# One decoder step on a Trainium2 core: two output tiles take turns, matmul by matmul, on one chunk of weights

## The chip, the cores and the metric

The kernel runs on one core of one Trainium2 chip. The metric is the device time of that core in microseconds; several executions are timed, and the median is given. Before the change it is 1397.88 us (3 runs, 1395.66 to 1398.28).

The engines in this text are TensorE (PE in the profile, with its weight loads as PEld), VectorE (DVE), ScalarE (ACT), GpSimd (POOL) and SyncE (SP), which issues most of the DMAs. PSUM is the memory into which TensorE adds; it is split into banks, and each accumulator of this kernel has a bank of its own.

## What is computed

One inference step of one decoder layer, for a prompt of 256 tokens and for 8 requests with 4 tokens each, 288 token columns in all. The model width is 2048, that of the feed-forward 5632.

```python
def layer(x, pos, ssm0, conv0, kbuf, vbuf, mk, mv, lp):
    mix, ssm_new, conv_new, k_new, v_new = mixer(rmsnorm(x, lp['norm_mix']), pos, ssm0, conv0, kbuf, vbuf, lp)
    x = x + mix
    x = x + cross_attn(rmsnorm(x, lp['norm_x']), mk, mv, lp)
    x = x + ffn(rmsnorm(x, lp['norm_ffn']), lp)
    return x, ssm_new, conv_new, k_new, v_new

def ffn(h, lp):
    return (jax.nn.silu(h @ lp['w_gate']) * (h @ lp['w_up'])) @ lp['w_down']
```

The mixer multiplies its input by `w_in`, and from the product come a gate, the inputs of a state-space scan (a causal convolution of four taps, then 16 heads with a state of 64 by 128 each) and queries, keys and values of a sliding-window attention with 16 heads. Both halves are joined and multiplied by `w_out`. The cross attention reads keys and values of 256 memory tokens. After the last layer comes a final norm. Everything is float32; besides the two outputs, the new states and caches are returned.

## The kernel before, in words

**Tiles.** Activations lie transposed: the 2048 channels are 16 tiles of 128 partitions, each with the 288 token columns. A matmul keeps a 128 x 128 slice of weights still and streams 288 columns of activations past it, into an accumulator `mm` of 128 x 288 in PSUM. float32 is reached by three matmuls of parts: weights and activations are each split into a rounded part (hi) and the rest (lo), and `mm3` (L164 to L168) adds lo·x_hi (L166), hi·x_hi (L167) and hi·x_lo (L168).

**Weights.** `wload` (L139 to L158) fetches a chunk of 128 x 1024 weights (512 KB) into a tile `raw` by SyncE's DMAs; ScalarE casts it to `hi` (L156), DVE subtracts to get `lo` (by the helper at L79). There are 3 buffers for raw, 4 for hi and 4 for lo. A chunk has four slices along the input channels (k) for two output tiles (m). In the chunks of the queries (`perm`), the two output tiles interleave in memory, and the split is done for each output tile apart, in two instructions of 512 columns each per engine; elsewhere one instruction splits the chunk.

**The order of the matmuls.** `gemm` takes accumulators for a pair of output tiles from a pool of four (`p_mm`) and has `gemm_w` (L179 to L189) go through the chunks:

```python
            for m in range(len(pss)):
                for k in range(n):
                    mm3(pss[m][:, :T], (hv[:, k, m * P:(m + 1) * P], lv[:, k, m * P:(m + 1) * P]), xs[k0 + k],
                        k0 + k == 0, k0 + k == nk - 1)
                if m == 0:
                    step(0)
```

So a full chunk gives 12 matmuls into the first accumulator, then 12 into the second. The next pair uses the other two accumulators. All large products go through it (input projection, output projection, cross attention's queries and output, feed-forward); only the memory keys and values call `mm3` themselves.

**Other work between them.** `later` puts a piece of work (a convolution, a part of the state-space scan, an attention step) into a queue with a due time, counted in chunks, and `step` (L127 to L132) emits what is due: once in the middle of a chunk, by `step(0)`, and once at its end. A scheduler then orders each engine's instructions by the priority of the place at which they were written; loads and splits are given a higher one, so that they run ahead.

**Places that the steps below touch.** `conv_pair` (L673 on) copies a tile of the input projection into a row with the old tail (L680 and L681 on GpSimd), scales it, and adds four taps (L82 on DVE); its tiles are called s, and the copy of the tail goes out as cc (L693, L694). `decay` makes masks m (L769 on DVE, a product at L79 on GpSimd). `ssd` makes four scaled copies of its input on GpSimd (L79, tiles s of 128 x 256), which `states` multiplies at L814 and L820. `sample_state` scales the old states (GpSimd, L79, tiles m from ld, 128 x 512). `residual` (L1011 on) adds a finished accumulator to the residual xT (DVE, L79), and squares the sum on ScalarE; at the very end, two tiles of squares wait in `tail` and are summed on TensorE by `final_sums` (L1275 to L1279). After that, TensorE transposes xT for the output (L118).

Of the kernel before, what the change touches and what calls it, by code (L numbers as in the profile page):

```python
# [15 lines left out]
P = 128  # L16
# [4 lines left out]
T = TP + TS  # L21
# [25 lines left out]
def tile_hymba_step(ctx: ExitStack, tc: tile.TileContext, I: dict, O: list, stop: int = 99):  # L47
    nc = tc.nc
# [3 lines left out]
    def tl(pool, shape, dt, tag):  # L52
        uid[0] += 1
        return pool.tile(shape, dt, name=f"{tag}_{uid[0]}", tag=tag)
# [20 lines left out]
    def acc():  # L75
        return tl(p_mm, [P, 512], F32, "mm")
# [49 lines left out]
    def step(n=1, part=False):  # L126
        clock[0] += n  # L127
        due = sum(t <= clock[0] for t, _, _ in pend)
        left = due // 2 if part else 0
        while pend and pend[0][0] <= clock[0] and (not part or due > left):  # L130
            due -= 1
            heapq.heappop(pend)[2]()  # L132
# [27 lines left out]
    def wslice(w, k0, nk, c0, ncol):  # L160
        v = w.rearrange("(k p) c -> p k c", p=P)
        return [(lambda r: r, v[:, k0:k0 + nk, c0:c0 + ncol])]

    def mm3(ps, w, x, start, stop):  # L164
        (wh, wl), (xh, xl) = w, x
        nc.tensor.matmul(ps, wl, xh, start=start, stop=False)  # L166
        nc.tensor.matmul(ps, wh, xh, start=False, stop=False)  # L167
        nc.tensor.matmul(ps, wh, xl, start=False, stop=stop)  # L168
# [5 lines left out]
    def gemm_part(pss, chunks, k0, nk, xs, ahead=AHEAD, perm=False):  # L174
        for pieces, n in chunks:
            gemm_w(pss, [wload(pieces, n, len(pss) * P, ahead, perm)], k0, nk, xs)
            k0 += n

    def gemm_w(pss, ws, k0, nk, xs):  # L179
        for hv, lv in ws:  # L180
            n = hv.shape[1]
            for m in range(len(pss)):
                for k in range(n):
                    mm3(pss[m][:, :T], (hv[:, k, m * P:(m + 1) * P], lv[:, k, m * P:(m + 1) * P]), xs[k0 + k],
                        k0 + k == 0, k0 + k == nk - 1)
                if m == 0:
                    step(0)
            k0 += n
        step(part=True)  # L189

    def gemm(chunks, nk, nm, xs, **kw):
        pss = [acc() for _ in range(nm)]
        gemm_part(pss, chunks, 0, nk, xs, **kw)
        return pss

    def kchunks(w, nk, c0, ncol, k_base=0):
        out = []
        k = 0
        while k < nk:
            n = min(1024 // ncol, nk - k)  # L200
            out.append((wslice(w, k_base + k, n, c0, ncol), n))
            k += n
        return out
# [116 lines left out]
    def ts(w=T, n=P, dt=F32):  # L320
        return tl(mxs, [P, 320], dt, "s")[:n, :w]
# [4 lines left out]
    def proj_in(c0, ncol):  # L326
        return gemm(kchunks(w_in, KC, c0, ncol), KC, ncol // P, xmix)

    # keys, values and the first queries
    wq = w_in.rearrange("(k p) c -> p k c", p=P)  # L330

    def q_chunk(rp, k0, nk=4):
# [74 lines left out]

    later(1, kv_natural)

    # dt path  # L410
    nat = ts(192).rearrange("p (c j h) -> p c j h", c=3, j=4)
    csrow = tc.dram_tile([16, T], F32, name="csrow")
    wdt = tl(p_ld, [P, 512], F32, "ld").rearrange("p (k h) -> p k h", h=32)
# [72 lines left out]
    later(1, dt_natural)  # L486
    later(7, dt_sums)

    # prompt sliding-window attention
    att = [(tl(p_xb, [P, T], F32R, "xb"), tl(p_xb, [P, T], F32R, "xb")) for _ in range(8)]  # L490
    qs = ts(256).rearrange("p (b r t) -> p b r t", r=8, t=4)
    mp = cst[:, C_MP:C_MP + 384]
# [69 lines left out]
        for m in range(2):  # L562
            swa_prompt(2 * rp + m, pq[m])

    # sample sliding-window attention
    def swa_sample():
        ms = cst[:, C_MS:C_MS + 144]
        kcT, vc = [], []
# [86 lines left out]
            cm.__exit__(None, None, None)  # L655
        return

    # state-space heads
    xc = [ts() for _ in range(12)]
    scT = ts().rearrange("p (c k) -> p c k", k=24)  # L660

# [178 lines left out]

        later(1, diag)

    # sample states
    bm = cst[:TS, C_BM:C_BM + 8]
    ssm = I["state_ssm"][0].rearrange("b (i f) p n -> i (f p) b n", f=2)
    osm = o_sssm[0].rearrange("b (i f) p n -> i (f p) b n", f=2)
# [79 lines left out]
        if jj % 2:  # L926
            later(4, lambda jj=jj: sample_state(jj // 2))

    # gate and group norm
    ymx = []  # L930

    def gate(i0, zzs, sqs):
# [21 lines left out]
    for g in range(2):  # L954
        sqs = ts()
        for zp in range(2):
# [7 lines left out]
            last = g == 1 and zp == 1  # L964
# [4 lines left out]
    def att_chunks(c0):  # L969
        chunks = []  # L970
        for j in range(2):
            pcs = []
            for g in range(2):
                r0 = 1024 + 512 * g + 256 * j
                pcs.append((lambda v, g=g: v[64 * g:64 * g + 64],
                            w_out[r0:r0 + 256, c0:c0 + 256].rearrange("(r d) c -> d r c", d=64)))
            chunks.append((pcs, 4))
        return chunks

    first = [[acc() for _ in range(2)] for _ in range(2)]  # L980
# [85 lines left out]
    for mp_ in range(8):  # L1066
        c0 = 256 * mp_
        if mp_ < 2:
            pss = first[mp_]
            gemm_part(pss, kchunks(w_out, 4, c0, 256, k_base=4), 12, KC, mix)  # L1070
        else:
            pss = gemm(att_chunks(c0) + kchunks(w_out, 8, c0, 256), KC, 2, mix)
# [5 lines left out]
    later(1, lambda: load_mem(2))  # L1078
    later(3, lambda: load_mem(3))

    # cross attention
    oT = [(tl(p_xb, [P, T], F32R, "xb"), tl(p_xb, [P, T], F32R, "xb")) for h in range(4)]
    qm = [ts(256).rearrange("p (b t) -> p b t", b=NB) for _ in range(4)]
    for h in range(4):
# [99 lines left out]
    for hp in range(2):  # L1184
# [6 lines left out]
        pss = gemm(kchunks(I["w_xq"][0], KC, 256 * hp, 256), KC, 2, xcs)  # L1191
# [37 lines left out]
    for w, o_ in ((I["w_xk"][0], o_pmk), (I["w_xv"][0], o_pmv)):  # L1229
        for hp in range(2):  # L1230
            pss = [acc() for _ in range(2)]
            for c in range(4):
                hv, lv = wload(wslice(w, 4 * c, 4, 256 * hp, 256), 4, 256)
# [30 lines left out]
    for mp_ in range(8):  # L1264
        pss = gemm(kchunks(I["w_xo"][0], 4, 256 * mp_, 256), 4, 2, oT)
# [1 line left out]
            residual(2 * mp_ + j, pss[j][:, :T], x3[2 * mp_ + j], V_F)  # L1267
    later(2, rstd_bcast)

    # feed-forward  # L1270
    NF = DFF // P
    NH = NF // 2

# [6 lines left out]
    for half in range(2):  # L1280
# [23 lines left out]
        for mp_ in range(8):  # L1304
            if half and mp_ == 7:
                later(3, lambda: final_sums(0, ssum))
            pss = gemm(kchunks(I["w_down"][0], NH, 256 * mp_, 256, k_base=half * NH), NH, 2, hs)
            for j in range(2):
                k = 2 * mp_ + j
# [5 lines left out]
                    if k == 0:  # L1315
                        act(rf[:, 13:14], xT[0][:, 0:1], AF.Sqrt, scale=0.0, bias=rf[:, 12:13])

    # final norm
    ydst = [o_yp[0, 0:P], o_yp[0, P:TP], o_ys.rearrange("b t d -> (b t) d")]
    ys = []  # L1320

# [108 lines left out]
```

## Time and profile before

| | before |
|---|---|
| median of 3 runs | 1397.88 us |
| lowest and highest | 1395.66 and 1398.28 us |
| span of the profiled execution | 1393.4 us |
| DMA | 241.17 MB, mean 173 GB/s |

The profile shows one execution of its own. For it no time beside its span is given; the span is the time from the first instruction to the last that the profiler recorded, and the median of the runs lies 4.48 us above it. An engine's busy time sums its instructions; since matmuls are pipelined, one begins before the one ahead of it has ended, and the spacing of starts tells more than the duration of one. PEclk is the clock that TensorE was granted as a share of full speed: 1.00 is 2.4 GHz and 0.50 is 1.2 GHz. In a timeline, the figure in brackets is the engine's idle time before the row, with what ended it.

### The profile page before, as it was taken

The numbers are of one execution on the slowest core, as the hardware profiler recorded it, in microseconds if no ns is written. First come the engines' busy times: TensorE is split into PE (matmuls) and PEld (weight loads), VectorE is DVE, ScalarE is ACT, GpSimd is POOL, SyncE is SP. The second block draws the span as 40 slices with busy tenths as digits, with TensorE's granted clock in tenths as the row PEclk, the third lists the DMA queues.
The fourth block names the chain that finished last, engine by engine and source line by source line (L and its number), as shares of the span: only waits on it lengthen the run. The fifth ranks groups of instructions, "written<-read, shape, count | busy, mean of one in ns | idle before, by whom it ended". The sixth has DMA issues, their size and how long they took to land.

```text
span 1393.4 us, 26184 instructions
## 1 busy us (share of the span) xinstructions
PE 1373.9 (99%) x10637; PEld 1338.3 (96%) x10637; DVE 809.1 (58%) x1341; ACT 635.1 (46%) x998; POOL 177.2 (13%) x273
## 2 busy tenths in 40 slices
PE   9899999999999999999999999999999999999997
PEld 8799988899998899999999999999999999999997
DVE  6777798766666559544544544444454554545554
ACT  6355776554555556433433433333343333434332
POOL 4311476403220113000000000000000000000110
PEclk9999999999999999999999999999999999999999
DMA  9655547667657745555555545555555555555552
GB/s 291 169 157 144 150 120 231 187 195 206 185 192 243 228 155 161 166 166 167 162 170 166 166 160 164 165 165 174 167 167 167 167 167 167 167 159 167 166 167 91
DMA packets 249856, 241.17 MB, mean 173 GB/s; under 512 B 12778, under 2 KB 240528, under 8 KB 249736
## 3 DMA queue, kind: packets, MB, share of 16 engines
q1 hardware_dynamic: 246120, 232.43, 54.9%
q0 software_dynamic: 3584, 7.06, 1.7%
q8 instruction: 83, 1.36, 0.4%
q14 instruction: 37, 0.30, 0.1%
q10 hardware_dynamic: 32, 0.01, 0.0%
HBM read 227.59 MB, written 11.85 MB: 172 GB/s over the span
## 4 chain that ended last, share of the span: by engine, by line
PE 87%; DVE 5%; DMA 2%; ACT 2%; issue 2%; POOL 0%; SPq 0%; DVEq 0%; ACTq 0%; POOLq 0%
PE mm L166 27%; PE mm L167 27%; PE mm L168 27%; PE ps L118 2%; DMA raw<-in_w_in_dram 2%; DVE lo L79 2%; DVE s L82 1%; ACT hi L156 1%; PE ps L511 1%; DVE xa L82 1%; DVE m L769 0%; PE ps L1134 0%; DVE s L79 0%; ACT L85 0%; ACT s L85 0%
## 5 line engine op out<-in xcount | busy, mean ns | idle before, releaser
L79 DVE TENSOR_TENSOR lo<-raw,hi 128x1024 fp32r<-128x1024 f32 (+1 forms) x413 | 483.0, 1172 | 472.7 <-ACT hi L156 466.3
L156 ACT CAST hi<-raw 128x1024 fp32r<-128x1024 f32 (+1 forms) x413 | 410.9, 998 | 547.4 <-PE mm L168 435.6
L166 PE MATMUL mm<-xa,lo 128*128 128x288 f32 x2016 | 601.2, 298 | 0.0
L167 PE MATMUL mm<-xa,hi 128*128 128x288 f32 x2016 | 597.5, 296 | 0.0
L168 PE MATMUL mm<-xa,hi 128*128 128x288 f32 x2016 | 591.0, 293 | 0.0
L166 PEld LDWEIGHTS mm<-xa,lo 128*128 128x128 f32 x2016 | 378.4, 188 | 4.7 <-issue 3.8
L168 PEld LDWEIGHTS mm<-xa,hi 128*128 128x128 f32 x2016 | 379.7, 188 | 0.7 <-issue 0.6
L167 PEld LDWEIGHTS mm<-xa,hi 128*128 128x128 f32 x2016 | 379.4, 188 | 1.0 <-issue 0.7
L79 POOL TENSOR_TENSOR ssum<-ssum,ls 128x288 f32<-128x288 f32 x43 | 46.9, 1091 | 880.0 <-ACT ls L85 879.1
L166 PE MATMUL mm<-ls,lo 128*128 128x288 f32 x512 | 152.0, 297 | 0.0
L168 PE MATMUL mm<-ls,hi 128*128 128x288 f32 x512 | 151.4, 296 | 0.0
L167 PE MATMUL mm<-ls,hi 128*128 128x288 f32 x512 | 151.1, 295 | 0.0
L167 PE MATMUL mm<-xb,hi 128*128 128x288 f32 x448 | 132.5, 296 | 0.0
L166 PE MATMUL mm<-xb,lo 128*128 128x288 f32 x448 | 132.1, 295 | 0.0
L168 PE MATMUL mm<-xb,hi 128*128 128x288 f32 x448 | 132.1, 295 | 0.0
L166 PEld LDWEIGHTS mm<-ls,lo 128*128 128x128 f32 x512 | 96.2, 188 | 0.1
L168 PEld LDWEIGHTS mm<-ls,hi 128*128 128x128 f32 x512 | 96.2, 188 | 0.0
L167 PEld LDWEIGHTS mm<-ls,hi 128*128 128x128 f32 x512 | 96.1, 188 | 0.1
L168 PEld LDWEIGHTS mm<-xb,hi 128*128 128x128 f32 x448 | 84.6, 189 | 0.2 <-DVE xb L79 0.2
L166 PEld LDWEIGHTS mm<-xb,lo 128*128 128x128 f32 x448 | 84.5, 189 | 0.1
L167 PEld LDWEIGHTS mm<-xb,hi 128*128 128x128 f32 x448 | 84.0, 188 | 0.1
L79 DVE TENSOR_TENSOR xT<-xT,mm 128x288 f32<-128x288 f32 x64 | 28.2, 448 | 39.1 <-PE mm L168 36.2
(304 smaller groups left out, 1211.3 us busy)
## 6 DMA issues: line engine op xcount, KB each, us to landing
raw<-in_w_gate_dram SPq DMA_DIRECT2D x88, 512.0 KB, 3.6
raw<-in_w_up_dram SPq DMA_DIRECT2D x88, 512.0 KB, 3.6
raw<-in_w_down_dram SPq DMA_DIRECT2D x80, 512.0 KB, 3.5
raw<-in_w_in_dram SPq DMA_DIRECT2D x43, 512.0 KB, 3.9
raw<-in_w_in_dram SPq DMA_DIRECT2D x34, 256.0 KB, 5.3
raw<-in_w_out_dram SPq DMA_DIRECT2D x32, 256.0 KB, 4.1
raw<-in_w_out_dram SPq DMA_DIRECT2D x16, 512.0 KB, 3.6
ld<-in_state_ssm_dram SPq DMA_DIRECT2D x16, 256.0 KB, 4.1
```

The source lines that it names most:

```text
L79: eng.tensor_tensor(out=out, in0=in0, in1=in1, op=op)
L82: nc.vector.scalar_tensor_tensor(out=out, in0=in0, scalar=s, in1=in1, op0=op0, op1=op1)
L118: nc.tensor.transpose(out, in_, ident[b:b + k, 0:k])
L156: nc.scalar.copy(h_, src)
L166: nc.tensor.matmul(ps, wl, xh, start=start, stop=False)
L167: nc.tensor.matmul(ps, wh, xh, start=False, stop=False)
L168: nc.tensor.matmul(ps, wh, xl, start=False, stop=stop)
L511: nc.tensor.matmul(pss[g][:, oc], qa[gs, qc], kT[gs, kc], start=True, stop=True)
```

## The change

In `gemm_w` the loop over the two output tiles goes inside: for each k and each of the three products, the matmul for the first accumulator is followed at once by the one for the second. The order of the three products for one accumulator, and its start and stop flags, stay. The queue's `step(0)` stood between the two output tiles; now it stands after the second of four values of k, again in the middle of the chunk. In a chunk with two values of k it stands after the first.

```diff
     def gemm_w(pss, ws, k0, nk, xs):
         for hv, lv in ws:
             n = hv.shape[1]
-            for m in range(len(pss)):
-                for k in range(n):
-                    mm3(pss[m][:, :T], (hv[:, k, m * P:(m + 1) * P], lv[:, k, m * P:(m + 1) * P]), xs[k0 + k],
-                        k0 + k == 0, k0 + k == nk - 1)
-                if m == 0:
+            for k in range(n):
+                xh_, xl_ = xs[k0 + k]
+                for w, x, first, last in ((lv, xh_, True, False), (hv, xh_, False, False), (hv, xl_, False, True)):
+                    for m in range(len(pss)):
+                        nc.tensor.matmul(pss[m][:, :T], w[:, k, m * P:(m + 1) * P], x,
+                                         start=first and k0 + k == 0, stop=last and k0 + k == nk - 1)
+                if k == (n - 1) // 2:
                     step(0)
             k0 += n
         step(part=True)
```

Behind these lines every line number grows by two (L814 becomes L816, L1277 becomes L1279). The scheduler moves other instructions with the matmuls; three places follow.

**TensorE, the last chunk of the last pair of output tiles.** mm_2607 and mm_2608 are the two accumulators, hi_2625 and lo_2626 the chunk's weights, ls the activations. Before:

```order
L166 MATMUL mm_2607_15543<-ls_2445_14266,lo_2626_15700 128x288
L167 MATMUL mm_2607_15543<-ls_2445_14266,hi_2625_15699 128x288
L168 MATMUL mm_2607_15543<-ls_2446_14267,hi_2625_15699 128x288
L166 MATMUL mm_2607_15543<-ls_2449_14276,lo_2626_15700 128x288
L167 MATMUL mm_2607_15543<-ls_2449_14276,hi_2625_15699 128x288
L168 MATMUL mm_2607_15543<-ls_2450_14277,hi_2625_15699 128x288
L166 MATMUL mm_2608_15544<-ls_2445_14266,lo_2626_15700 128x288
L167 MATMUL mm_2608_15544<-ls_2445_14266,hi_2625_15699 128x288
L168 MATMUL mm_2608_15544<-ls_2446_14267,hi_2625_15699 128x288
L166 MATMUL mm_2608_15544<-ls_2449_14276,lo_2626_15700 128x288
L167 MATMUL mm_2608_15544<-ls_2449_14276,hi_2625_15699 128x288
L168 MATMUL mm_2608_15544<-ls_2450_14277,hi_2625_15699 128x288
```

And now:

```order
L186 MATMUL mm_2607_15543<-ls_2445_14266,lo_2626_15700 128x288
L186 MATMUL mm_2608_15544<-ls_2445_14266,lo_2626_15700 128x288
L186 MATMUL mm_2607_15543<-ls_2445_14266,hi_2625_15699 128x288
L186 MATMUL mm_2608_15544<-ls_2445_14266,hi_2625_15699 128x288
L186 MATMUL mm_2607_15543<-ls_2446_14267,hi_2625_15699 128x288
L186 MATMUL mm_2608_15544<-ls_2446_14267,hi_2625_15699 128x288
L186 MATMUL mm_2607_15543<-ls_2449_14276,lo_2626_15700 128x288
L186 MATMUL mm_2608_15544<-ls_2449_14276,lo_2626_15700 128x288
L186 MATMUL mm_2607_15543<-ls_2449_14276,hi_2625_15699 128x288
L186 MATMUL mm_2608_15544<-ls_2449_14276,hi_2625_15699 128x288
L186 MATMUL mm_2607_15543<-ls_2450_14277,hi_2625_15699 128x288
L186 MATMUL mm_2608_15544<-ls_2450_14277,hi_2625_15699 128x288
```

The first accumulator's last matmul was the sixth from the end and is the second from the end now; in a chunk with four values of k it goes from the thirteenth from the end to the second. Behind these matmuls, the column sums of the second tile of squares (L1279 now) stand three transposes (L118) later than they did (L1277).

**TensorE, at the products of `states` in the mixer** (ps from s; xa, hi and lo belong to the input projection, cst is the identity). Before:

```order
L166 MATMUL mm_507_2525<-xa_15_136,lo_534_2651 128x288
L814 MATMUL ps_527_2637<-s_513_2560,s_434_2155 128x256
L820 MATMUL ps_529_2641<-s_434_2155,s_514_2562 128x128
L820 MATMUL ps_529_2641<-s_435_2156,s_515_2564 128x128
L820 MATMUL ps_529_2641<-s_434_2155,s_514_2562 128x128
L820 MATMUL ps_529_2641<-s_435_2156,s_515_2564 128x128
L167 MATMUL mm_507_2525<-xa_15_136,hi_533_2650 128x288
L168 MATMUL mm_507_2525<-xa_31_152,hi_533_2650 128x288
L118 MATMUL ps_535_2679<-cst_82,s_304_1495 128x128
```

And now:

```order
L186 MATMUL mm_507_2525<-xa_32_153,hi_542_2694 128x288
L186 MATMUL mm_506_2524<-xa_17_138,lo_543_2695 128x288
L186 MATMUL mm_507_2525<-xa_17_138,lo_543_2695 128x288
L816 MATMUL ps_527_2637<-s_513_2560,s_434_2155 128x256
L822 MATMUL ps_529_2641<-s_434_2155,s_514_2562 128x128
L822 MATMUL ps_529_2641<-s_435_2156,s_515_2564 128x128
L822 MATMUL ps_529_2641<-s_434_2155,s_514_2562 128x128
L822 MATMUL ps_529_2641<-s_435_2156,s_515_2564 128x128
L118 MATMUL ps_535_2679<-cst_82,s_304_1495 128x128
```

L814, which is L816 now, stood inside the chunk of hi_533 and lo_534, behind 934 large matmuls; it stands inside the next chunk (hi_542, lo_543) now, behind 944. The transposes of s_304 still follow behind 936 before, 944 now.

On DVE, the split of that next chunk, lo_543, has moved with it. The piece of the difference there (s_499 is the second convolution tile, m_522 a mask of the scan, xb the keys and values):

```order
-L79 TENSOR_TENSOR lo_534_2651<-raw_532_2649,hi_533_2650 128x1024
-L79 TENSOR_TENSOR xb_157_720<-ps_480_2359,xb_156_719 128x32
-L82 SCALAR_TENSOR_TENSOR s_499_2509<-s_498_2508,cwT_111,s_499_2509 128x312
-L769 TENSOR_SCALAR m_522_2590<-csb_519_2584,s_137_679 128x128
-L82 SCALAR_TENSOR_TENSOR s_499_2509<-s_498_2508,cwT_111,s_499_2509 128x312
+L79 TENSOR_TENSOR lo_543_2695<-raw_541_2693,hi_542_2694 128x1024
 L79 TENSOR_TENSOR xb_159_722<-ps_480_2359,xb_158_721 128x32
 L82 SCALAR_TENSOR_TENSOR s_499_2509<-s_498_2508,cwT_111,s_499_2509 128x312
-L79 TENSOR_TENSOR lo_543_2695<-raw_541_2693,hi_542_2694 128x1024
```

The split lo_543 now stands ahead of all three taps of s_499; lo_534, xb_157 and m_522 stand earlier in the changed program.

**GpSimd, around the second convolution tile.** s_498 is that tile with its old tail, cc_500 the tail that goes out, m_579 to m_582 the scaled old states of `sample_state`, s_513 the first of the four copies for `states`. Before:

```order
L680 MEMSET s_498_2508 128x3
L681 COPY s_498_2508<-s_314_1505 128x8x3
L689 MEMSET s_499_2509 128x3
L693 COPY cc_500_2521<-s_498_2508 128x3
L694 COPY cc_500_2521<-s_498_2508 128x24
L79 TENSOR_TENSOR m_579_2850<-ld_549_2741,s_413_2024 128x512
L79 TENSOR_TENSOR m_580_2852<-ld_550_2743,s_413_2024 128x512
L79 TENSOR_TENSOR m_581_2854<-ld_551_2745,s_473_2320 128x512
L79 TENSOR_TENSOR m_582_2856<-ld_552_2747,s_473_2320 128x512
L79 TENSOR_TENSOR s_513_2560<-s_486_2440,s_137_679 128x256
```

And now:

```order
L79 TENSOR_TENSOR m_522_2590<-m_522_2590,s_440_2175 128x512
L79 TENSOR_TENSOR m_579_2850<-ld_549_2741,s_413_2024 128x512
L79 TENSOR_TENSOR m_580_2852<-ld_550_2743,s_413_2024 128x512
L79 TENSOR_TENSOR m_581_2854<-ld_551_2745,s_473_2320 128x512
L682 MEMSET s_498_2508 128x3
L683 COPY s_498_2508<-s_314_1505 128x8x3
L691 MEMSET s_499_2509 128x3
L79 TENSOR_TENSOR m_582_2856<-ld_552_2747,s_473_2320 128x512
L695 COPY cc_500_2521<-s_498_2508 128x3
L696 COPY cc_500_2521<-s_498_2508 128x24
L79 TENSOR_TENSOR s_513_2560<-s_486_2440,s_137_679 128x256
```

The copy into s_498 stood ahead of the four products of the old states and stands behind three of them now, and behind the product m_522, which stood behind s_513 and the other three copies before.

## Rows read from the trace of the kernel before

**Rows 1.** The page: its head and part 1, busy time by engine.

```profile
span 1393.4 us, 26184 instructions
...
PE 1373.9 (99%) x10637; PEld 1338.3 (96%) x10637; DVE 809.1 (58%) x1341; ACT 635.1 (46%) x998; POOL 177.2 (13%) x273
```

**Rows 2.** Table by stages: window, us, busy us by engine, PEclk, DMA share, GB/s.

```profile
190.00:250.00 60.00, 53.30 (x436) 46.93 (x436) 53.36 (x82) 39.60 (x71) 41.78 (x56) 0.94 0.61 175
...
545.00:1379.00 834.00, 833.93 (x6298) 833.56 (x6297) 411.84 (x496) 317.38 (x376) 15.30 (x14) 1.00 0.53 163
```

**Rows 3.** The same table, the stretch behind the wait.

```profile
195.00:201.50 6.50, 5.35 (x19) 4.20 (x20) 6.45 (x6) 2.41 (x5) 6.36 (x6) 0.50 0.56 163
```

**Rows 4.** Timeline of PE at the wait: start, us, engine, line, operation, tiles, count.

```profile
192.72 0.29 PE L166 MATMUL mm<-xa,lo 128*128 128x288 f32 x1
195.06 1.22 PE L814 MATMUL ps<-s,s 128*128 128x256 f32 x2 [2.04 <-POOL s L79]
...
199.85 0.44 PE L168 MATMUL mm<-xa,hi 128*128 128x288 f32 x1
200.09 0.63 PE L118 MATMUL ps<-cst,s 128*128 128x128 f32 x2
```

**Rows 5.** Timeline of PE in the first and the last of 169 uninterrupted chunks.

```profile
562.51 0.29 PE L168 MATMUL mm<-xa,hi 128*128 128x288 f32 x1
562.64 0.30 PE L166 MATMUL mm<-xa,lo 128*128 128x288 f32 x1
...
563.30 0.29 PE L168 MATMUL mm<-xa,hi 128*128 128x288 f32 x1
563.44 0.30 PE L166 MATMUL mm<-xa,lo 128*128 128x288 f32 x1
...
1236.78 0.29 PE L168 MATMUL mm<-xa,hi 128*128 128x288 f32 x1
1236.91 0.30 PE L166 MATMUL mm<-xa,lo 128*128 128x288 f32 x1
```

**Rows 6.** Timeline of all engines, at a chunk of the queries.

```profile
37.38 2.49 DVE L79 TENSOR_TENSOR lo<-raw,hi 128x512 fp32r<-128x512 f32 x4
...
40.06 0.40 PE L166 MATMUL mm<-xa,lo 128*128 128x288 f32 x1
```

**Rows 7.** Timeline of all engines, behind the last large matmul.

```profile
1378.62 0.45 DVE L79 TENSOR_TENSOR xT<-xT,mm 128x288 f32<-128x288 f32 x1 [9.64 <-PE mm L168]
...
1379.42 0.45 DVE L79 TENSOR_TENSOR xT<-xT,mm 128x288 f32<-128x288 f32 x1 [0.35 <-PE mm L168]
...
1379.79 0.36 DVE L1314 TENSOR_SCALAR xT<-xT,vT 128x288 f32<-128x288 f32 x1
...
1381.38 0.50 PE L118 MATMUL ps<-cst,xT 128*32 128x128 f32 x3
...
1381.72 0.49 PE L118 MATMUL mm<-cst,xT 128*128 128x128 f32 x3
```

**Rows 8.** Timeline of POOL, ahead of the wait.

```profile
186.34 0.42 POOL L681 COPY s<-s 128x24 f32<-128x24 f32 x1
...
188.26 0.19 POOL L693 COPY cc<-s 128x3 f32<-128x3 f32 x1 [1.48 <-DVE s L79]
...
188.55 5.65 POOL L79 TENSOR_TENSOR m<-ld,s 128x512 f32<-128x512 f32 x4
194.16 4.96 POOL L79 TENSOR_TENSOR s<-s,s 128x256 f32<-128x256 f32 x4
```

**Rows 9.** Timeline of DVE, ahead of the wait.

```profile
189.80 1.23 DVE L82 SCALAR_TENSOR_TENSOR s<-s,cwT,s 128x312 f32<-128x312 f32 x1
190.95 1.07 DVE L769 TENSOR_SCALAR m<-csb,s 128x128 f32<-128x128 f32 x1
...
194.46 1.63 DVE L79 TENSOR_TENSOR lo<-raw,hi 128x1024 fp32r<-128x1024 f32 x1
```

**Rows 10.** Timeline of ACT at the wait.

```profile
194.57 0.54 ACT L85 ACTIVATE s<-s 128x256 f32<-128x256 f32 x2 [0.31 <-DVE s L82]
```

## The prediction

> **What bounds the kernel now.** I read the page first, for its busy times, then a table by stages, then the order of instructions in time at the places where TensorE (PE) is not busy. The page gives PE 1373.9 us of a span of 1393.4 us, and one weight load for each of 10637 matmuls [rows 1]; the loads lie beside the matmuls, so PE's own stream is the candidate. The stages confirm it: from 545 us to 1379 us PE is busy for 833.93 of 834.00 us at full granted clock, while VectorE (DVE) has 411.84 us to do. Only between 190 and 250 us does PE stand for longer, 6.7 us of 60 [rows 2]. So two things can move the time: the spacing of matmuls in the long stream, and a few waits in the mixer.
>
> The spacing: 834.00 us by 6298 matmuls is 132.4 ns each [rows 2]. A matmul streams 288 columns. Where the granted clock stands at 0.50, 1.2 GHz, the next start comes 0.24 us after a big matmul's (199.85 to 200.09) [rows 3, 4], which is 288 columns at 1.2 GHz and nothing more. At 2.4 GHz 288 columns take 120 ns, so 12.4 ns of each matmul are not columns. The change can pay in a large way only if those 12.4 ns come from adding to the same PSUM bank twice in a row.
>
> **The bank change is already in the trace.** Before, the 24 matmuls of a chunk change bank twice: after the 12th, and with the next chunk. Elsewhere neighbours add to the same bank. In the stretch 560 to 1380 us I took the 169 chunks whose moving operand is xa and which nothing interrupts; [rows 5] hold starts of the first and of the last of them. From the 12th matmul to the 13th, where the bank changes, starts lie 132.5 ns apart on the mean; from the 6th to the 7th and from the 18th to the 19th (338 of them), between the same two instructions with the bank kept, 132.5 ns too. The means differ by less than 0.1 ns. In the first chunk one reads 562.51 to 562.64 (kept) and 563.30 to 563.44 (changed), in the last 1236.78 to 1236.91 (changed): the hundredths come from rounding, and the same step reads 0.14 once and 0.13 once. A stall between neighbours in one bank would be missing at each of these changes. It is not missing.
>
> **Part by part.**
>
> 1. *Turns between banks.* By the program's order, neighbouring matmuls of this routine in different banks rise from 717 to 8683, 7966 more. At under 0.1 ns each that is under 0.8 us in either direction; I take 0.
>
> 2. *Other order of operands.* Before, the slice of hi was loaded twice in a row (for x's hi and x's lo part); now two slices take turns. Loads stay one per matmul [rows 1]. Before, only L168 repeats its neighbour's slice, and six matmuls take 0.79 us with two such repeats among them (562.51 to 563.30) [rows 5], 0.132 us each like the whole stretch; I take 0, as PE's stream covers the loads. If the cover went, PE would show idle time before loads.
>
> 3. *Both tiles need their weights at once.* In the query chunks (perm) the split of the second tile's half is a separate instruction, and PE could spend 12 matmuls, 1.6 us, on the first tile meanwhile. Now the second matmul needs it. In the tightest of the 16 such chunks four splits run from 37.38 to 39.87 us; the two for this chunk are the first two, done by 38.7 us by their share, and PE starts the chunk at 40.06 us [rows 6]. A cover of 1.4 us is left: cost 0. Without it one half split, 0.6 us, would be paid per chunk, 16 times at most.
>
> 4. *Evictions at the end of a pair.* The first tile was complete 12 matmuls before the second in a full chunk; now both end together. In the stream this is covered: the next pair has two other banks, its matmuls take at least one chunk, 24 x 0.132 = 3.2 us, and an eviction takes 0.45 us [rows 7]. The Trainium skill speaks against the change here: "Perfetto Trace Analysis", section Optimizing Tensor Performance, says that independent groups should rotate through banks so that one group's evacuation runs beside the next group's matmuls. The turns give that up inside a pair; as the pairs rotate as well, the trace makes it cost nothing but at the end of the kernel, where by the rule alone the whole eviction would be added.
>  At the end no pair follows. Before, the first tile's eviction starts at 1378.62 and the second's at 1379.42 [rows 7]. Now the first starts one matmul earlier than that, 1379.29, holds DVE for 0.37 us (to 1379.79 for the second before), and the second starts at 1379.66: +0.24 us. PE also runs three transposes ahead of the second set of column sums that stood behind them; they take 0.34 us (1381.38 to the next at 1381.72), and the last scale factors wait for these sums. The squares that these sums read come 0.24 us later, the sums themselves start 0.34 us later, so the two don't add: **+0.3 us**, bounds 0.24 and 0.58.
>
> 5. *Instructions that the new order moves.* Nearly all small matmuls keep their place among the big ones. The exception that meets a wait is L814 (with its L820): 934 big matmuls stood ahead of it, now 944. There PE waits 2.04 us for GpSimd (POOL) [rows 4]. POOL starts the four products that L814 and L820 want at 194.16 us [rows 8] whatever PE does. So ten matmuls, 10 x 0.132 = 1.3 us, go into the wait: **-1.3 us**. The eight of them that belong to the next chunk need its lo split. Before, that split ran at 194.46 on DVE, behind work that began at 189.80; now most of that work stands behind it, but for one operation of 1.07 us. So it should start near 190.9 and be done some 1.6 us later, near 192.5, by the length that it had [rows 9]. PE wants it at 193.0 (192.72 and two matmuls). If it came late, the gain would shrink, to 0 at worst.
>  Others moved by 9 at most (the next L814 to 1034 from 1043): 1.2 us either way, taken as 0 because PE does not wait at them now.
>
> Sum: 0 + 0 + 0 + 0.3 - 1.3 = -1.0 us. The execution shown has a span of 1393.4 us, so 1392.4 us. The median of the runs, 1397.88 us, lies 4.48 us above that span; with the same distance, **1396.9 us**. The case's own range, from terms 4 and 5 and the 1.2 us, is 1395.6 to 1399.7 us. About 0.2%, 2.8 us, is what a measurement of this kernel can tell from no change.
>
> **Rivals.**
>
> *A. The bank is the limit after all.* Then all of the 12.4 ns goes in 8928 matmuls: -111 us, 1287 us. For it: the 12.4 ns exist at full clock and not at half, as a limit outside the array would look. Against it: [rows 5]. It could only be true if one change of bank in twelve were too rare to help.
>
> *B. The clock stays up at 195 us.* The granted clock is 0.50 from 195.0 to 201.5 [rows 3], after PE had stood for most of 192.72 to 195.06 [rows 4]. PE was busy for 5.35 us of these 6.5; at full clock half of that goes, -2.7 us on top of -1.0: 1394.2 us. Against it: POOL still ends its four products no earlier, so PE still stands.
>
> *C. POOL's queue turns against it (slower).* On POOL three of the four long products of the state update (1.41 us each, four in 5.65 us at 188.55) and one shorter product now stand ahead of the short copy of the second convolution tile, which ran at 186.34 [rows 8]. ScalarE, DVE and in the end PE's transposes of that tile at 200.09 [rows 4] hang on it; ScalarE wrote the tile from 194.57 [rows 10], five us early. If the copy comes more than these 5 us later, each further us is one of PE. With two of the products too many, 2.8 us, with 1.4 us more of half clock, and the tail: 1397.9 + 0.3 + 2.8 + 1.4 = 1402.4 us. For it: the queue has moved just there, and POOL is busy for 6.36 of 6.5 us at 195 us [rows 3]. Against it: POOL was idle for 1.48 us before 188.26 [rows 8], which the new order fills.
>
> *D. Cycling costs clock (slower).* In the trace the clock is full wherever banks change every twelfth matmul. Should turns at every matmul make it fall, each per cent of the 8928 matmuls at 0.24 instead of 0.132 us costs 9.6 us: 1407 us for one per cent, without a bound near by. The Trainium skill tells of this in "TensorE: Matmul & The Clock Gate", section A second HAM failure mode: psum-queue depth-cycling, for a kernel that went from bank to bank each iteration. By that rule this rival would be likely; the trace does not agree so far, with 1.00 over 834 us [rows 2].
>
> That the change would not be in force is excluded: the built program shows the turns.
>
> **How the numbers follow.** The forecast gets 0.62: the stream's spacing is measured at the very event that the change multiplies, and what remains are waits of a us or two. B 0.15, A 0.04, C 0.16, D 0.03. Faster by over 0.2% (under 1395.1 us) are A and B, 0.19; slower (over 1400.7 us) C and D, 0.19; within 0.62. The range takes in B and C, 1393.8 to 1402.5 us, and leaves out A and D.
>
> **What would show it.** Right: spacing stays 132 ns in 545 to 1379 us; the wait at L814 shrinks by about 1.3 us; the last sums end some 0.3 us later after the last big matmul. Wrong: spacing under 131 or over 134 ns in the long stream (A, D), a clock row without the second fall (B), or transposes of s_304 and s_305 waiting for ScalarE (C).

## The result, and the profile after

The changed kernel is slower: 1401.53 us (median of 20 runs, 1398.19 to 1404.17) against 1396.26 us (20 runs of the kernel before on the same chip, 1391.81 to 1400.44). The ratio is 1.0038, with an interval of 1.0027 to 1.0049, so 5.3 us more where 1.0 us less had been forecast. (The forecast started from 1397.88 us, the median of three runs; twenty runs of the same kernel give 1396.26.) The profiled execution took 1402.63 us, 2.1 us above its span. From its page:

```profile
span 1400.5 us, 26184 instructions
...
PE 1379.2 (98%) x10637; PEld 1339.8 (96%) x10637; DVE 813.3 (58%) x1341; ACT 628.5 (45%) x996; POOL 171.7 (12%) x273
```

The table by stages (window, us, busy us by engine, PEclk, DMA share, GB/s) answers to [rows 2]:

```profile
60.00:190.00 130.00, 126.98 (x992) 117.00 (x990) 96.14 (x306) 78.96 (x186) 33.05 (x68) 0.93 0.48 137
190.00:250.00 60.00, 53.74 (x460) 47.59 (x458) 51.69 (x88) 37.61 (x70) 43.34 (x62) 1.00 0.61 173
...
545.00:1379.00 834.00, 833.87 (x6276) 830.58 (x6276) 419.41 (x501) 316.46 (x381) 18.12 (x16) 1.00 0.53 164
```

In the long stream PE is as busy as before, at full clock, and still starts 22 matmuls fewer in 834 us (6276, not 6298): 2.9 us. Between 60 and 190 us it is granted 0.93 of its clock.

Both programs have 10637 matmuls, so the same matmul can be looked up by its number in either trace. The table gives the time between the starts of numbered ones, for the two kernels and the eight experiments, each in its one profiled execution, and beside it the ratio of the timed runs. "Mixer" runs from the span's start to number 2600, "xo" from 4182 to 4290 (the end of the cross attention's output), "FFN" from 4290 to 10500, just ahead of the last large ones. "Scores" is a part of the mixer, from 1100 to 1200, around the second half of the sample scores. "Half clock" is the time at 0.50 inside the mixer.

| kernel | mixer | scores | half clock | xo | FFN | ratio (interval) |
|---|---|---|---|---|---|---|
| before | 339.6 | 11.0 | 10.2 | 14.95 | 822.2 | 1 |
| changed | 342.5 | 18.2 | 17.1 | 16.63 | 825.0 | 1.0038 (1.0027 to 1.0049) |
| e1: turns in the FFN only | 338.2 | 11.0 | 10.2 | 14.93 | 825.1 | 1.0024 (1.0012 to 1.0036) |
| e2: turns up to xo only | 342.5 | 15.7 | 17.1 | 14.97 | 819.5 | 0.9999 (0.9984 to 1.0013) |
| e3: changed, gates out first | 342.0 | 15.4 | 13.7 | 16.64 | 821.6 | 1.0026 (1.0011 to 1.0041) |
| e4: changed, last chunk apart | 340.0 | 12.5 | 17.1 | 14.95 | 821.5 | 1.0004 (0.9988 to 1.0019) |
| e5: changed, cache copied late | 334.6 | 11.0 | 10.2 | 16.64 | 825.1 | 1.0008 (0.9996 to 1.0021) |
| e6: before, cache copied late | 336.9 | 11.0 | 10.2 | 14.93 | 822.2 | 0.9984 (0.9973 to 0.9995) |
| e7: e4 and e5 together | 340.4 | 11.0 | 17.1 | 14.96 | 821.5 | 0.9973 (0.9959 to 0.9987) |
| e8: e2, cache copied late | 337.2 | 11.0 | 13.7 | 14.92 | 819.6 | 0.9957 (0.9942 to 0.9972) |

The loss lies in three places: 2.8 us in the FFN, 1.7 us at xo, 2.9 us in the mixer, 7.4 us in all, where the two spans differ by 7.1 (the stretch between takes 0.4 us less, the end 0.1 us more). The first two come back in every kernel that has the turns in that place; the mixer's share changes from execution to execution. Its 2.9 us is what is left of a loss of 7.2 us at the scores and a lead of 4.4 us that the changed kernel has at matmul 1100. The lead can't be put down to the turns. It comes from a wait near 56 us (L511 before, L513 now), where 4.4 us lie between two starts before the change and 1.8 us in the changed kernel, but 3.7 us in e2, which has the same order up to there; and from 3.4 us of half clock at 61.8 us, behind that wait, which the changed kernel's profile doesn't show. Over the 20 runs of the changed kernel the mean granted clock goes from 0.991 to 0.995; the three runs at 0.995 take 1398.19 to 1399.21 us, those at 0.991 and 0.992 take 1400.48 to 1404.17.

**The FFN.** The spacing is what it was: 132.2 ns on the mean between uninterrupted matmuls of the gate and up products, before and after. What is new stands at the first matmuls of each gate pair, 22 times. The timeline of all engines at one of them (start, us, engine, line, operation, tiles, count, idle before with its releaser):

```profile
569.26 0.29 PE L186 MATMUL mm<-xa,lo 128*128 128x288 f32 x1
569.33 0.82 DVE L79 TENSOR_TENSOR ls<-mm,rb 128x288 f32<-128x288 f32 x2 [0.69 <-PE mm L186]
569.39 0.43 PE L186 MATMUL mm<-xa,hi 128*128 128x288 f32 x2
...
569.65 0.58 PE L186 MATMUL mm<-xa,lo 128*128 128x288 f32 x2
...
570.08 0.43 PE L186 MATMUL mm<-xa,hi 128*128 128x288 f32 x2
```

From 569.65 to 570.08 are 0.43 us for two matmuls that elsewhere take 0.26 (569.39 to 569.65): starts 186 and 237 ns apart, 0.158 us lost. The program's order on the two engines tells what is waited for. mm_1571 and mm_1572 are the gate's two tiles, mm_1585 and mm_1586 those of up, mm_1607 and mm_1608 the next gate's, in the first pair's banks again:

```
DVE  L79 TENSOR_TENSOR ls_1600_7869<-mm_1585_7746,rb2_924_4369 128x288 [waits PE_49]
DVE  L79 TENSOR_TENSOR ls_1603_7878<-mm_1572_7625,rb2_924_4369 128x288
PE   L186 MATMUL mm_1607_7888<-xa_1411_6706,lo_1611_7892 128x288
PE   L186 MATMUL mm_1608_7889<-xa_1409_6704,lo_1611_7892 128x288 [waits DVE_49]
```

The gate's second tile has been complete for 96 matmuls, but in DVE's queue it is taken out behind the first tile of up, and that tile is complete only with the pair now. Before, it was complete 12 matmuls earlier, and the second bank was wanted 12 matmuls later. In the trace of the kernel before, the same two evictions begin 1.1 us ahead of the new pair's first matmul (565.42), and the starts go on 0.13 us apart:

```profile
564.33 0.82 DVE L79 TENSOR_TENSOR ls<-mm,rb 128x288 f32<-128x288 f32 x2
...
565.42 0.29 PE L166 MATMUL mm<-xa,lo 128*128 128x288 f32 x1
...
565.55 0.29 PE L167 MATMUL mm<-xa,hi 128*128 128x288 f32 x1
...
565.68 0.29 PE L168 MATMUL mm<-xa,hi 128*128 128x288 f32 x1
```

**The cross attention's output (xo)** has one chunk for each pair. From the same view:

```profile
538.31 0.81 DVE L79 TENSOR_TENSOR xT<-xT,mm 128x288 f32<-128x288 f32 x2
...
538.80 0.77 PE L186 MATMUL mm<-xb,lo 128*128 128x288 f32 x2 [0.15 <-DVE xT L79]
...
539.03 1.21 DVE L79 TENSOR_TENSOR lo<-raw,hi 128x1024 fp32r<-128x1024 f32 x1
...
540.17 2.06 DVE L82 SCALAR_TENSOR_TENSOR xa<-xT,vT,xa 128x288 fp32r<-128x288 f32 x2
...
542.15 0.80 DVE L79 TENSOR_TENSOR xT<-xT,mm 128x288 f32<-128x288 f32 x2
```

A pair costs DVE 3.84 us (538.31 to 542.15, without a break) and PE 24 x 0.132 = 3.17 us, so DVE falls behind from pair to pair, and PE comes to wait for its banks. Before, DVE had the same work and hardly a break either (busy for 17.81 of the 18 us from 525 to 543 us), but the first tile's eviction could begin 11 matmuls earlier, and PE did not come to wait.

**The mixer.** All engines, ahead of the second half of the sample scores (L597):

```profile
142.48 3.09 POOL L583 DMA_DIRECT2D out_dram<-m  x2 [15.04 <-DMA m<-in_cache_swa_v_dram]
...
145.74 0.11 POOL L691 MEMSET s<- 128x3 f32 x1
...
145.86 0.65 ACT L85 ACTIVATE s<-s,vT,cwT 128x312 f32<-128x312 f32 x1 [4.95 <-POOL s L691]
...
146.41 1.98 ACT L156 CAST hi<-raw 128x1024 fp32r<-128x1024 f32 x2
146.54 1.12 DVE L82 SCALAR_TENSOR_TENSOR s<-s,cwT,s 128x312 f32<-128x312 f32 x2 [6.34 <-ACT s L85]
...
150.73 0.36 DVE L601 CUSTOM_DVE_ANT_0 m<-ps,cst,hvec 128x144 f32<-128x144 f32 x1
...
151.15 0.44 PE L597 MATMUL ps<-m,s 64*32 64x128 f32 x4 [3.02 <-DVE stx L601]
```

GpSimd issues the copies of two cache tiles to the output (L583), and holds its queue for 15 us until their load has landed. Behind them stands the memset and copy for a convolution tile; ScalarE waits 4.95 us for those, with two casts of weights behind that; DVE waits 6.34 us for ScalarE, with splits and the reading of the scores behind that; PE waits 3.02 us. Then the clock is at half (150.00:160.50):

```profile
150.00:160.50 10.50, 9.35 (x49) 8.09 (x50) 5.21 (x25) 8.41 (x21) 2.46 (x7) 0.51 0.50 155
```

In the kernel before, GpSimd stood as long, but ScalarE had one cast (144.22) ahead of the convolution tile in its queue and DVE got its split, and ScalarE's wait for GpSimd was 0.47 us:

```profile
144.22 1.05 ACT L156 CAST hi<-raw 128x1024 fp32r<-128x1024 f32 x1 [2.07 <-issue]
...
146.08 1.57 POOL L581 DMA_DIRECT2D out_dram<-m  x1 [14.82 <-DMA m<-in_cache_swa_v_dram]
...
147.83 0.11 POOL L689 MEMSET s<- 128x3 f32 x1
...
147.95 0.65 ACT L85 ACTIVATE s<-s,vT,cwT 128x312 f32<-128x312 f32 x1 [0.47 <-POOL s L689]
```

The column "scores" of the table holds what this costs at its place: 11.0 us in the kernel before, 18.2, 15.7 and 15.4 us in the three profiles with full turns in the mixer and the copies where they were (changed, e2, e3), so 4.4 to 7.2 us, the half clock included.

### The profile page after: what moved, and what is told of

It is laid out like the page before. It is cut to its first block, busy times and chain, and to the rows that moved or that the text cites. A ratio compares the mean times of both kernels' runs of the same rounds, so it can differ in the third digit from the quotient of the medians.

```text
span 1400.5 us, 26184 instructions
## 1 busy us (share of the span) xinstructions
PE 1379.2 (98%) x10637; PEld 1339.8 (96%) x10637; DVE 813.3 (58%) x1341; ACT 628.5 (45%) x996; POOL 171.7 (12%) x273
## 4 chain that ended last, share of the span: by engine, by line
PE 90%; DVE 4%; issue 2%; DMA 1%; ACT 1%; POOL 1%; SPq 0%; DVEq 0%; ACTq 0%; POOLq 0%
PE mm L186 79%; PE ps L118 3%; PE mm L166 1%; DVE lo L79 1%; PE mm L167 1%; PE mm L168 1%; DVE s L82 1%; DVE xa L82 1%; POOL m L79 0%; ACT hi L156 0%; PE ps L513 0%; DMA raw<-in_w_in_dram 0%; PE ps L1136 0%; DMA m<-in_cache_swa_v_dram 0%; DMA raw<-in_w_out_dram 0%
## 5 line engine op out<-in xcount | busy, mean ns | idle before, releaser
L186 PE MATMUL mm<-xa,hi 128*128 128x288 f32 x4032 | 706.4, 296 | 0.0
L186 PEld LDWEIGHTS mm<-xa,hi 128*128 128x128 f32 x4032 | 596.9, 188 | 1.1 <-issue 0.7
L186 PE MATMUL mm<-xa,lo 128*128 128x288 f32 x2016 | 442.7, 298 | 0.2 <-DVE xT L79 0.2
L186 PEld LDWEIGHTS mm<-xa,lo 128*128 128x128 f32 x2016 | 326.4, 189 | 8.0 <-issue 3.8
L186 PE MATMUL mm<-ls,hi 128*128 128x288 f32 x1024 | 177.4, 295 | 0.0
L186 PE MATMUL mm<-xb,hi 128*128 128x288 f32 x896 | 156.1, 295 | 0.0
L186 PEld LDWEIGHTS mm<-ls,hi 128*128 128x128 f32 x1024 | 149.8, 188 | 0.0
L186 PE MATMUL mm<-ls,lo 128*128 128x288 f32 x512 | 111.0, 297 | 0.0
L118 PE MATMUL ps<-cst,ld 128*128 128x128 f32 (+2 forms) x228 | 38.4, 276 | 1.2 <-DVE m L79 1.2
L166 PE MATMUL mm<-hi,xa 128*128 128x256 f32 x128 | 37.9, 296 | 0.0
L167 PE MATMUL mm<-hi,xa 128*128 128x256 f32 x128 | 36.7, 286 | 0.0
```

Source lines behind the costliest of these rows:

```text
L118: nc.tensor.transpose(out, in_, ident[b:b + k, 0:k])
L186: nc.tensor.matmul(pss[m][:, :T], w[:, k, m * P:(m + 1) * P], x, start=first and k0 + k == 0, stop=last and k0 + k == nk - 1)
```

## The experiments

The theories: (1) evictions that come late cost the time in the FFN and at xo; (2) the mixer's waits and its clock cost it; (3) the turns slow each matmul.

**e1 and e2: turns in one part of the program only.** `gemm_w` has both loops, and a flag chooses; it is set at the heading of the feed-forward (e1), or cleared ahead of the cross attention's output (e2).

```diff
+            if turns[0]:
+                for k in range(n):
...
+            else:
                 for m in range(len(pss)):
```

> Turns only in the feed-forward; everything ahead of it in the order of the kernel before. Theory 1 (late evictions): in each of the 22 gate/up pairs TensorE waits some 0.16 us for the bank of the gate's second tile, 22 x 0.158 = 3.5 us, and the end costs 0.3 us: 3.8 us over the kernel before, a ratio near 1.0027, and the profile shows 22 double gaps (about 185 and 237 ns between starts) at the first matmuls of a new gate tile. Theory 2 (the mixer's waits and its half clock make the loss): no change from the kernel before, within 1 us. Theory 3 (turns slow each matmul): more than 132.5 ns between uninterrupted matmuls.

Measured: 1397.87 us against 1394.71, ratio 1.0024 (1.0012 to 1.0036), 3.3 us. The double gaps are there, all 22. Theory 1 holds for the FFN; theory 3 falls, since the spacing of the others is 132.2 ns. The 0.3 us expected at the end can't be told there (below).

> Turns in the mixer, the output projection and the cross attention's queries; the order of the kernel before in the cross attention's output and the feed-forward. Theory 1: what the profile of the changed kernel shows up to 530 us, 2.5 us, is mostly the chance of one execution; the median is between 0 and 2.5 us over the kernel before, ratio 1.000 to 1.0018, and no double gaps in the feed-forward. Theory 2: the whole loss, 5 us, ratio 1.0037, and a clock share under that of the kernel before.

Measured: 1395.51 us, ratio 0.9999, no double gaps. It looked as if the mixer cost nothing. The table says otherwise: the mixer is 2.9 us longer in the profiled execution, just as in the changed kernel (4.7 us longer at the scores), but the FFN, in the order of before, is 2.7 us *shorter* (the last section has what is known of it). In that execution the two cancel, and the time alone would have misled.

**e3: VectorE's order in the FFN.**

```diff
+            gs = [ts() for _ in range(2)]
+            for j in range(2):
+                tt(nc.vector, gs[j], pg[j][:, :T], rb2, ALU.mult)
+                act(gs[j], gs[j], AF.Silu)
             for j in range(2):
-                gg, uu = ts(), ts()
-                tt(nc.vector, gg, pg[j][:, :T], rb2, ALU.mult)
-                act(gg, gg, AF.Silu)
+                gg, uu = gs[j], ts()
```

> The changed kernel, with one edit in the feed-forward: both tiles of the gate are taken out of PSUM ahead of the first tile of up in VectorE's queue (the order was gate 0, up 0, gate 1, up 1; now gate 0, gate 1, up 0, up 1). Theory 1: the 22 double gaps go, 3.5 us less than the changed kernel, 1398 us by the 1401.5 of its runs; what is left over the kernel before is the cross attention's output (1.6 us) and the mixer's. Theory 1b (it is the accumulator as such, not the queue): the gaps stay, 1401.5 us. Theory 2: 1401.5 us.

Measured: 1398.65 us against 1394.71, ratio 1.0026 (1.0011 to 1.0041) where the changed kernel has 1.0038. These two intervals overlap, so the timed runs don't settle it; the trace does: no double gap is left, and the FFN takes 821.6 us, not 825.0, 3.4 us less where 3.5 were expected. At the same place as above, in the timeline of all engines:

```profile
568.86 0.82 DVE L79 TENSOR_TENSOR ls<-mm,rb 128x288 f32<-128x288 f32 x2 [0.69 <-PE mm L186]
...
569.05 0.69 PE L186 MATMUL mm<-xa,hi 128*128 128x288 f32 x4
569.58 0.42 PE L186 MATMUL mm<-xa,lo 128*128 128x288 f32 x2
```

Only up's tiles are left to take out when the pair ends, and the first matmuls of the new pair take turns 0.13 us apart. So it is the place in DVE's queue, not the bank as such: theory 1b falls. The gaps at xo stay (16.64 us).

**e4: the last chunk of each product in the old order.**

```diff
-            for k in range(n):
+            if k0 + n < nk:
+                for k in range(n):
...
+            else:
+                for m in range(len(pss)):
...
```

> The changed kernel, but in the last chunk of every product one output tile is finished ahead of the other, as before; turns in all other chunks. Theory 1: no double gaps in the feed-forward and none of the gaps at the cross attention's output (which has a single chunk for each product), 3.5 + 1.6 + 0.3 us less than the changed kernel: 1396 us, the kernel before within 1 us. Theory 2: 1401 us. Theory 3 (turns slow each matmul): over five of six large matmuls still take turns, so most of the loss stays.

Measured: 1395.53 us against 1394.71, ratio 1.0004 (0.9988 to 1.0019). No double gaps, and xo takes 14.95 us as before. Theory 1 accounts for both places; three of four large matmuls of gate and up still take turns (the expectation had their share too high), so theory 3 is out.

**e5 and e6: the cache's copy late in GpSimd's queue**, in the changed kernel (e5) and in the kernel before (e6). The two DMAs are issued in `combine`, and ordered behind GpSimd's last copy of the convolution tiles written by then.

```diff
-            nc.gpsimd.dma_start(o_sv[0, 4 * hb:4 * hb + 4, 0:124].rearrange("b t g d -> t b (g d)"),
-                                v_[4:128].rearrange("p (b c) -> p b c", b=4))
+            vouts.append(v_)
...
         def combine(pts2):
+            with tc.issue_after(behind[0].ins):
+                for hb, v_ in enumerate(vouts):
+                    nc.gpsimd.dma_start(o_sv[0, 4 * hb:4 * hb + 4, 0:124].rearrange("b t g d -> t b (g d)"),
+                                        v_[4:128].rearrange("p (b c) -> p b c", b=4))
```

> The changed kernel, with the two DMAs that copy the old values of the cache out (issued by GpSimd, which waits for their load to land) put behind GpSimd's copies for the convolution tiles that they stood ahead of. Theory A (GpSimd's queue): ScalarE's wait of 4.95 us for GpSimd's memset near 141 us goes below 1 us, with it VectorE's wait of 6.3 us and TensorE's of 3.0 us at the second half of the sample scores, and the half clock behind it (10.2 us from 150 us) goes or shrinks; the mixer up to the products of w_out takes some 3 us less, the kernel 1398 us (1396.5 to 1399.5 by the 1401.5 of the changed kernel). Theory B (the order of VectorE's and ScalarE's own work is what is late): TensorE still stands for over 2 us there, 1401 us.

Measured: 1397.46 us against 1396.88, ratio 1.0008 (0.9996 to 1.0021). From the timeline of e5, the same instructions, and its stage row:

```profile
140.80 0.10 POOL L696 MEMSET s<- 128x3 f32 x1
140.94 0.63 ACT L85 ACTIVATE s<-s,vT,cwT 128x312 f32<-128x312 f32 x1
141.48 1.03 ACT L156 CAST hi<-raw 128x1024 fp32r<-128x1024 f32 x1
141.61 1.12 DVE L82 SCALAR_TENSOR_TENSOR s<-s,cwT,s 128x312 f32<-128x312 f32 x2 [1.29 <-ACT s L85]
...
148.18 0.42 PE L598 MATMUL ps<-m,s 64*32 64x128 f32 x8
```

```profile
150.00:160.50 10.50, 10.50 (x87) 9.60 (x86) 8.01 (x28) 8.81 (x18) 4.29 (x7) 1.00 0.16 60
```

ScalarE doesn't wait, DVE 1.29 us, PE not at all; 87 matmuls where the changed kernel started 49, and the scores take 11.0 us, not 18.2. Theory A holds for the place. In time the edit is worth 0.30% by the ratios, 4.2 us, where some 3 were expected. The profiles show more than that: the mixer is 7.9 us shorter. But e5's profiled execution, 1395.02 us, lies 2.4 us under its median, and that of the changed kernel 1.1 us above its own.

> The same edit in the kernel before. Theory A: ScalarE waits only 0.47 us for GpSimd there before the change, so the kernel before gains nothing, ratio 0.999 to 1.001. Theory B says the same. If instead it gains 2 us or more, GpSimd's stop cost the kernel before something too, and less of the difference between the two kernels goes to its account.

Measured: 1394.29 us, ratio 0.9984 (0.9973 to 0.9995): a gain of 2.2 us by the ratio, where none was expected. By the expectation, GpSimd's stop would then have cost the kernel before something too. Its profiled execution doesn't show where: the scores take 11.0 us with the edit and without it, and of the 2.7 us by which its mixer is shorter, 1.7 lie ahead of matmul 400, at the wait near 56 us that differs among all these kernels. That stays open. The edit is worth 0.30% in the changed kernel and 0.16% here; the difference, 2.0 us, would be this queue's part of the change's loss, but it is inside the uncertainty of the three ratios.

**e7 and e8: the edits together.**

> The changed kernel with both edits: one output tile finished ahead of the other in the last chunk of each product, and the cache's copy late on GpSimd. If late evictions and GpSimd's queue are all that the turns cost, it is the kernel before within 1 us (ratio 0.9993 to 1.0007), with no wait over 1 us at the sample scores and no double gaps in the feed-forward; if the turns themselves brought something that the two costs hid, it is faster by over 1.5 us.

Measured: 1391.59 us, ratio 0.9973 (0.9959 to 0.9987), 3.8 us under the kernel before by the ratio. There are no double gaps and no wait at the sample scores (11.0 us), as expected. The expected tie is missed. By the expectation's own words the turns would then have brought something, but 2.2 us of this are e6's gain, which has no turns in it; the rest is inside the uncertainty. Its profiled execution, 1395.64 us, is its slowest of 12, so its mixer of 340.4 us is not its usual one.

> Turns in the mixer, output projection and the cross attention's queries only, with the cache's copy late on GpSimd. Theory A: the mixer loses its 3 us, so it is 2 to 3 us under the same kernel without the edit (which was the kernel before within its interval): ratio 0.998 to 0.999. It also asks whether the shorter spacing of that kernel's second half of the feed-forward (131.1 ns for each matmul where all other kernels have 132.2, for an unchanged order) comes back: if it belongs to the built kernel, it need not; if not, 132.2 ns.

Measured: 1390.46 us against 1396.88, ratio 0.9957 (0.9942 to 0.9972): the lowest ratio here, and under both kernels. Against e2 the edit is worth 0.42%, more than the 0.1 to 0.2% expected, and the scores take 11.0 us, not 15.7. The shorter spacing comes back. Of the 0.27% by which e8 lies under e6, 2.6 us are that spacing; what is left for turns in the mixer is about 1 us, inside the uncertainty.

## Why the prediction was wrong

- **Terms 1 and 2 (turns, operands): right.** The change of bank is worth nothing and the reordered loads cost nothing: 132.2 ns before and after. Rival A falls as [rows 5] had it.
- **Term 3 (query chunks): right.** No new wait stands there; matmul 300, behind the first ones, starts 0.3 us earlier than before (the ten profiles differ by 1.3 us there).
- **Term 4 (evictions): this is the step that failed.** "In the stream this is covered: the next pair has two other banks, its matmuls take at least one chunk, 24 x 0.132 = 3.2 us, and an eviction takes 0.45 us" counts one eviction and the time until its own bank is wanted. It does not ask what the eviction of the *other* pair, whose bank is wanted at once, stands behind in DVE's queue (the FFN: 22 x 0.158 = 3.5 us, less the 0.7 us by which the FFN is shorter in e3 and e4 too; 2.8 us by the traces, 3.3 us by e1's runs), nor whether DVE has 3.2 us left for a pair (xo: it needs 3.84; 1.7 us). Both could be read beforehand: the order of the evictions in DVE's queue, and DVE's rows at xo. By the rule of the Trainium skill that was weighed there ("Perfetto Trace Analysis", section Optimizing Tensor Performance) this speaks against the change in the stream too. The trace agrees in so far as the double gaps came with the turns; but e3 keeps the turns and has no such gap, so what costs is the place of the eviction in its queue.
- **The end, +0.3: later at the sums, not at the end.** Both evictions did go together (1386.27, 0.82 us for two). The last column sums start 2.33 us after the last large matmul (1386.07), 1.72 us before the change (1379.08): the two shifts did add, to 0.6 us. But the step that waits for these sums, on ScalarE, had stood behind a copy (L1330) before; now that copy is done earlier. Before, then after:

```profile
1380.80 0.66 PE L1277 MATMUL ps<-cst,ls 128*128 128x1 f32 x6
...
1381.92 0.58 ACT L1330 COPY ld<-ps 32x512 f32<-32x512 f32 x1 [1.05 <-PE ps L118]
...
1382.41 0.29 ACT L85 ACTIVATE rf<-rf 128x4 f32<-128x4 f32 x1
```

```profile
1388.40 0.66 PE L1279 MATMUL ps<-cst,ls 128*128 128x1 f32 x6
1388.60 0.57 ACT L1332 COPY ld<-ps 32x512 f32<-32x512 f32 x1 [0.56 <-PE ps L118]
...
1389.30 0.30 ACT L85 ACTIVATE rf<-rf 128x4 f32<-128x4 f32 x1
```

  That step starts 3.33 us behind the last large matmul before and 3.23 us now. From number 10570 to the span's end it is 15.26 us, 15.15 before; over the ten profiles it is 15.12 to 15.55 us with the old order there and 15.20 to 15.36 us with turns, so no cost can be told.
- **Term 5 (L814, -1.3): near the size at the wait, in part by luck, and given back behind it.**

```profile
200.51 0.70 PE L816 MATMUL ps<-s,s 128*128 128x256 f32 x2 [1.01 <-POOL s L79]
...
202.87 0.94 PE L822 MATMUL ps<-s,s 128*128 128x128 f32 x6 [1.06 <-POOL s L79]
...
208.99 0.66 PE L835 MATMUL ps<-s,s 128*64 128x128 f32 x8 [2.14 <-ACT s L818]
```

  2.04 us became 1.01 [rows 4]. But the term let POOL start the four products at 194.16 us whatever PE does; they started at 199.40, and PE came to L816 6.5 us later than to L814 before. That the difference comes out near the forecast is luck. Behind it, ScalarE's copy for L835 came late, 2.14 us. That "Others moved by 9 at most" costs 0 was argued from PE alone; that ScalarE's convolution tile moved ahead of a cast of weights, near 141 us, was in the order too.
- **Rival C (GpSimd's queue) had the engine, not the place.** It was put at 188 us with the products of the old states as the price; it came at 142 us through two DMA issues that wait for a load, and cost 4.4 to 7.2 us at the scores in the profiled executions. Its 1402.4 us is near the time for a reason that was only half its own. The transposes that it named do wait for ScalarE in e5 (2.20 us at 197.94), but not in the changed kernel.
- **Rivals B and D.** The half clock at 195 us did go (and 3.4 us of it near 62 us), but 10.2 us at 150 and 6.8 us at 174 came in its place (17.1 us, 10.2 before). Rival D is out: 1.00 over the 834 us in which nearly every neighbour changes bank. In the section of the Trainium skill named there ("TensorE: Matmul & The Clock Gate", section A second HAM failure mode: psum-queue depth-cycling) the clock goes up and down because TensorE is idle for short times between groups of matmuls. Here it was busy for 833.87 of these 834.00 us, so the run does not test that rule; it shows that turns alone cost no clock.

By parts the profiles give 2.8 + 1.7 + 2.9 us; the timed runs give 5.3 (3.8 to 6.8). The first two are shown by e1, e3 and e4. They leave 0.8 us (-0.7 to 2.3) of the timed loss for the mixer; e5 and e6 give it 2.0 us, inside the uncertainty. The mixer's mechanism is shown at its place by e5 and e8; how much of it the kernel's usual time holds stays open.

## What to carry to other kernels

In this kernel a bank came free when the eviction had had its turn in DVE's queue, not when the tile was complete (96 matmuls lay between): before two accumulators are made to end together, read what stands ahead of each eviction, and whether the evicting engine has time for a pair at all. A change of matmul order also moves small work between the queues; follow it through the engines that issue DMAs, since one issue that waits for a load held up everything behind it (15 us here). And compare stretches between the same instructions: in e2 a loss of 2.9 us hid behind a gain of 2.7, and in the changed kernel's mixer a loss of 7.2 us hid behind a lead of 4.4 that the turns don't account for.

## What the runs showed that was not expected

The same matmuls in the same order run at two spacings. In e8 (and in e2) the gate and up products of the second half take 131.1 ns each, those of the first half 132.2; in the kernel before both take 132.2. The tables by stages of e8, then of the kernel before:

```profile
600.00:800.00 200.00, 200.00 (x1515) 200.00 (x1514) 101.30 (x127) 78.00 (x95) 0.00 (x0) 1.00 0.54 166
1000.00:1200.00 200.00, 200.00 (x1527) 200.00 (x1527) 101.52 (x128) 79.03 (x96) 0.00 (x0) 1.00 0.54 167
```

```profile
1000.00:1200.00 200.00, 200.00 (x1515) 200.00 (x1514) 101.31 (x127) 77.79 (x94) 0.00 (x0) 1.00 0.54 166
```

Within a stretch the spacings repeat, to within the rounding: in the slower one with a period of six matmuls (131.7, 133.3, 132.5, 132.5, 137.5, 125.8 ns), in the faster one, in e8, with a period of nine (132.0, 131.1, 131.9, 131.0, 133.0, 130.0, 126.0, 131.0, 134.0 ns). What puts TensorE's stream into the one or the other was not found; it came in both programs that have turns up to xo and the old order behind, and in none of the other eight. It is 2.6 us, twice the largest term of the prediction.
